# Placement matrices, norm rows and warm-up products of a mixture-of-experts stage set between the gate and up products

## The chip, the cores and the metric

One core of one Trainium2 chip runs the whole program. The metric is device time in microseconds (us) of one execution, lower is better. TensorE is called PE in the rows, its weight loads PEld, VectorE DVE, ScalarE ACT, GpSimd POOL, and the queue that issues the transfers SP.

## The reference, cut to what matters

Two post-norm layers over 512 tokens of width 1024. Layer 0 mixes tokens with attention, layer 1 with window pooling; each is followed by a mixture of 32 experts, where every token goes to two experts of one group of eight.

```python
for i in range(DEPTH):                       # DEPTH = 2
    mix = diff_attention(h, ...) if i % 2 == 0 else pool_mixer(h, ...)
    h = layer_norm(DEEPNORM_ALPHA * h + mix, ln_g[i, 0], ln_b[i, 0])
    ffn = hier_moe(h, ...)
    h = layer_norm(DEEPNORM_ALPHA * h + ffn, ln_g[i, 1], ln_b[i, 1])
...
def run_block(args):                         # one block of tokens of one expert
    xb, e = args
    h = jax.nn.silu(xb @ w_gate[e]) * (xb @ w_up[e])
    return h @ w_down[e]
...
out = jnp.zeros((N, D), x.dtype).at[tok_pad].add(y * w_pad[:, None])
```

## The kernel before

Each layer has a mixer stage and a mixture stage; the change is in the mixture stage, the function `moe` (lines 865 to 1250), which is called once for each layer. The 32 experts are taken as 16 pairs. An expert has 64 token slots, so a pair fills the 128 rows of a tile. The stage runs eight rounds, q = 0 to 7, of two pairs each (the loop at line 1160): the first pair of a round is p = 2q, the second p = 2q + 1. The order of PE's instructions in it is the order of the code (a manual schedule); DVE, ACT and POOL are ordered by a list scheduler that works on a cost model, so code that is moved on PE also moves work in their queues.

A pair goes through these steps. `gate_up` (L938) multiplies the gathered tokens `xT` with the gate weights into the PSUM bank psg and with the up weights into psu; ACT makes `sg`, the silu of psg (L945), DVE the product `h` with psu (L947). `flip` transposes h on PE (tp, L952), ACT copies it to hT (L953), and `down` (L963) multiplies it with the down weights into y. ACT (L972) and DVE (L973) split y, weighted by the slot weights `ws`, into a high and a low part `yy`. Later `spread_all` (L1130 to L1142) adds the rows back to their tokens: for each of 4 token tiles and 2 column halves a product of the placement matrix `Sm` with yy goes into a PSUM tile "sc" (four products for the two pairs of a round), and DVE adds the tile to the residual sum r (L1142). The spread of a round's two pairs stands in the next round, behind the gate and up products of its first pair: column half 0, then the flip, then column half 1.

`Sm` and `ws` of a pair come from `places` (L907): four transposes of the one-hot matrix G on PE (ga, L912), a copy by ACT to Sm (L913), four narrow products (pw, L916), and on DVE a copy pwc (L918) and two additions (L921). In this kernel both pairs of a round have this done one after the other, right ahead of the first pair's down product. Sm has three buffers. Behind the second pair's up product `gather2` makes the next round's G on DVE (L566, L567) and gathers its tokens on PE (L897) in four rounds of two column blocks, which ACT (L881) and DVE (L883) copy to xT; the flip stands between the second and the third of them.

Two more steps are rare. In round 0 `residue` (L1115) builds rows of the first norm's gains and shifts (row, L379) and scales r with them on DVE (L1121, L1123): four rows, behind the gather. In round 7 `norm_rows` (L383) builds four rows for the second norm, each copied by ACT to gb (L385), behind the spread.

PSUM has eight banks here: psg and psu (pool p0), and in pool p1 "ga", "tp" and the two banks of y, one buffer each; pool p2 has two buffers of the tag "sc". The gather's tiles go to "ga" and "tp" in turn, pw and the flip use "tp", the norm rows "sc" or "ga".

SP issues the weight transfers, 1 MB each, in the order of use; `fill` lets it run ahead by up to 14 units, and a transfer starts when the unit that it overwrites has been read.

`warm` (L302) is a helper that issues n products of constants, 128 x 256 in bf16, which nothing reads.

Of the kernel before, what the change touches and what calls it, by code (L numbers as in the profile page):

```python
# [8 lines left out]
F32 = mybir.dt.float32  # L9
F32R = mybir.dt.float32r  # L10
# [29 lines left out]
WARM3 = 24  # L40
WARM4 = 10
WARM2 = 2
REGION = {mybir.EngineType.PE, mybir.EngineType.DVE, mybir.EngineType.Activation, mybir.EngineType.Pool}
FILL2 = 3

# [19 lines left out]
def tile_trunk(ctx, tc, x, w_qkv, w_o, p_in, p_grp, p_scale, p_out,  # L65
# [804 lines left out]
    def moe(l, rt_in, name1, after):  # L870
        with ExitStack() as es:
# [13 lines left out]
            def gather(slots, cc, xT, pairs):  # L885

                n = pairs * P
                G = keep.tile([P, NT, 2 * P], F32R, name="G", tag="G")
                for j in range(NT):
                    do(place_in(G[:, j, 0:n], slots, cc, j))  # L890

                def round(k0, ga):
                    for k in range(k0, k0 + 2):
                        for j in range(NT):
                            g = G[:, j] if pairs == 2 else G[:, j:j + 1, 0:P].to_broadcast([P, 2, P])
                            for i in range(2):
                                PE.matmul(ga[:, k - k0], half_of(xs[j], i).bitcast(F32R)[:, k], g,  # L897
                                          start=j + i == 0, stop=j + i == NT)
                    for k in range(k0, k0 + 2):
                        factor(xT[:, k, 0:n], ga[:, k - k0, 0:n], k, (ACT, V)[k % 2])  # L900

                def ga_tile(k0):
                    return p1.tile([P, 2, 2 * P], F32, name="ga", tag=("ga", "tp")[k0 // 2 % 2])

                return G, [lambda k0=k0: round(k0, ga_tile(k0)) for k0 in range(0, KD, 2)]

            def places(G, i, wd, Sm, ws):  # L907

                ga = p1.tile([P, NT, P], F32, name="ga", tag="ga")
                gi = G[:, :, i * P:(i + 1) * P]  # L910
                for j, t in enumerate(tiles):
                    PE.transpose(ga[:, t], gi[:, j].bitcast(F32), ident)  # L912
                ACT.activation(Sm[:, :].rearrange("p (t q) -> p t q", t=NT), ga, AF.Copy)  # L913
                pw = p1.tile([P, 4], F32, name="pw", tag="tp")
                for t in range(NT):
                    PE.matmul(pw, gi[:, t], wd[:, t], start=t == 0, stop=t == NT - 1)  # L916
                pc = mo.tile([P, 4], F32, name="pwc", tag="pwc")
                V.tensor_copy(pc, pw)  # L918
                for e in range(2):
                    es_ = slice(e * CAP, (e + 1) * CAP)  # L920
                    V.tensor_tensor(ws[es_], pc[es_, e:e + 1], pc[es_, 2 + e:3 + e], op=OP.add)  # L921

            def run(todo):
                if todo:
# [133 lines left out]
            plc = {}  # L1058

            def place(G, p):  # L1060
                Sm = mo.tile([P, S], F32R, name="Sm", tag="Sm", bufs=3)
                ws = mo.tile([P, 1], F32, name="ws", tag="ws", bufs=3)
                places(G, p % 2, wd[:, :, p], Sm, ws)
                plc[p] = Sm, ws

            def seek(xT1, Sm1):

# [18 lines left out]
                V.tensor_scalar(rem, rem, 0.0, None, op0=OP.max)  # L1086
                G1, rounds = gather(sl, code, xT1, 1)
                do(rounds)
                places(G1, 0, wx, Sm1, ws1)

            def fetch(w, pr, u2):
                wv = w[l].rearrange("e (p k) n -> e p (k n)", p=P)
# [9 lines left out]
                        nc.sync.dma_start(u2[c][e], wv[bass.ds(pr[e], 1), :, :, c * 512:(c + 1) * 512]  # L1102
                                          .rearrange("a p k n -> (a p) k n"))

            def bank():
                return p1.tile([P, 512], F32, name="row", tag="ga")

            def whole(c):

                for j, t in enumerate(tiles):  # L1110
# [1 line left out]
                    hi, lo = [half_of(xs[j], i)[:, :, c * 64:(c + 1) * 64] for i in range(2)]  # L1112
                    nc.gpsimd.tensor_tensor(rq, hi, lo, op=OP.add)

            def residue(q, tag):  # L1115

                ps = norm_row(l, 0, q, p2.tile([P, 512], F32, name="row", tag=tag))
                for t in tiles:
                    r = tok(R, t)[:, q % 2 * 512:(q % 2 + 1) * 512]
                    if q < 2:  # L1120
# [9 lines left out]
            def spread_all(c, ys):  # L1130

                for t in range(NT):
                    spread_sum([(yr, Sm) for yr, Sm in ys], t, c)
# [7 lines left out]
                r = tok(R, t)[:, c * 512:(c + 1) * 512]  # L1141
                V.tensor_tensor(r, r, ps, op=OP.add)  # L1142

            def gate_of(p):
                h = h_tile()
                gate_up(xT[:, :, (p % 2) * P:(p % 2 + 1) * P],
                        [[take(nm, l, p, e) for e in range(2)] for nm in "gu"], h)
                done(8)
                return h

# [9 lines left out]
            for q in range(NPAIR // 2):  # L1160
                p, final = 2 * q, q == NPAIR // 2 - 1

                fill(CAPW)
                h = gate_of(p)
                if q == 0:
                    R = two("r")
                    whole(0)
# [2 lines left out]
                fill(CAPW)  # L1170
                if prev:
                    spread_all(0, prev)
                hT = hT_tile()
                flip(h, hT)
                if prev:
                    spread_all(1, prev)
                if final:
                    gb, rows_ = norm_rows(l, 1, bank)
                    do(rows_)
                place(G, p)  # L1180
                place(G, p + 1)
                prev = [down_of(p, hT, wdn)]

                p += 1
                fill(5 if final else CAPW)
                h = gate_of(p)
                wdn = [take("d", l, p, i) for i in range(2)]
                Sm, ws = plc[p]
                if final:
# [16 lines left out]
                else:  # L1206
                    fill(CAPW)
                    xT, (G, rounds) = gather2(p + 1)
                    rows_ = [lambda i=i: residue(i, "sc") for i in (0, 2, 1, 3)] if q == 0 else []
                    do(rounds[0:2])  # L1210
                    hT = hT_tile()
                    flip(h, hT)
                    do(rounds[2:4] + rows_)
                    prev.append(down_of(p, hT, wdn))


# [107 lines left out]
```

## Time and profile before

| what | before |
|---|---|
| device time, median of 3 runs | 1577.65 us (1576.52 to 1577.86) |
| the profiled execution | 1577.44 us, span 1575.7 us |
| mean granted TensorE clock | 0.968 of full speed |
| PE busy | 1463.4 us (93% of the span) |
| DVE, ACT, POOL busy | 623.4 us (40%), 366.9 us (23%), 82.0 us (5%) |
| HBM traffic | 285 GB/s over the span |

The span runs from the first to the last instruction of the profiled execution; the device time has 1.7 us around it. A busy share is the share of the span in which an engine executed something. The granted clock is 1.00 at 2.4 GHz and 0.50 at 1.2 GHz. The two mixture stages stand at about 310 to 875 us and 1031 to 1553 us.

### The profile page before, as it was taken

Reading aid. Unit: us, or ns where it says so; the run is one execution under the profiler, and the core shown is the slowest. Engines: PE = TensorE matmul, PEld = TensorE weight load, DVE = VectorE, ACT = ScalarE, POOL = GpSimd, SP = SyncE. Lnnn points to the kernel's source line nnn. Section 1 sums busy time; section 2 is a strip of 40 time slices with the busy share of each in tenths; the row PEclk is TensorE's granted clock in tenths of the full one; section 3 lists DMA queues with packets and bytes.
Section 4 is the critical chain, followed back from the end, with each engine's and each line's share of the span. In section 5 each row is a group of like instructions: output and inputs, shape, how many; then the busy total and the mean of one; then the engine's idle time right before and its main releaser. Section 6 shows DMA issues by size and latency. Waiting matters only on the chain. (4 is left out here: it accounts for less than half of the span.)

```text
span 1575.7 us, 18863 instructions
## 1 busy us (share of the span) xinstructions
PE 1463.4 (93%) x7477; PEld 840.2 (53%) x7477; DVE 623.4 (40%) x1441; ACT 366.9 (23%) x738; POOL 82.0 (5%) x52
## 2 busy tenths in 40 slices
PE   9999999998999999999998599998999999999993
PEld 7767777734544454445542377844455445444541
DVE  4366466643331322322233866653322213313216
ACT  4355464511111111111110423421111011111110
POOL 0000000320000000000000600230000000000001
PEclk9999999999999999999899799999999999999987
DMA  7111431677999999999866016467999999999921
GB/s 258 38 54 55 160 134 55 267 316 294 413 397 409 411 408 399 412 406 411 337 267 229 13 54 241 196 266 295 413 408 411 397 408 413 399 407 413 406 104 55
DMA packets 85570, 450.19 MB, mean 286 GB/s; under 512 B 10648, under 2 KB 20448, under 8 KB 36320
## 3 DMA queue, kind: packets, MB, share of 16 engines
q1 hardware_dynamic: 85472, 448.86, 71.3%
q8 instruction: 64, 1.05, 0.3%
q14 instruction: 34, 0.28, 0.1%
HBM read 446.74 MB, written 2.10 MB: 285 GB/s over the span
## 5 line engine op out<-in xcount | busy, mean ns | idle before, releaser
L963 PE MATMUL y<-w_d,hT 128*64 128x512 f32 x960 | 226.3, 627 | 0.0
L938 PE MATMUL psg<-w_g,xT 128*64 128x512 f32 x1024 | 225.2, 593 | 0.2 <-ACT xT L881 0.2
L938 PE MATMUL psu<-w_u,xT 128*64 128x512 f32 x1024 | 225.1, 592 | 0.0
L973 DVE SCALAR_TENSOR_TENSOR yy<-y,ws,yy 128x512 fp32r<-128x512 f32 x66 | 48.6, 737 | 397.1 <-ACT yy L972 382.4
L938 PEld LDWEIGHTS psu<-w_u,xT 128*64 128x64 f32 x1024 | 73.1, 137 | 146.6 <-issue 142.9
L938 PEld LDWEIGHTS psg<-w_g,xT 128*64 128x64 f32 x1024 | 72.9, 137 | 146.0 <-issue 141.6
L963 PEld LDWEIGHTS y<-w_d,hT 128*64 128x64 f32 x960 | 69.3, 144 | 132.9 <-issue 131.1
L897 PEld LDWEIGHTS ga<-G,xs 128*128 128x128 f32 x960 | 114.1, 188 | 12.2 <-issue 12.2
L897 PE MATMUL ga<-G,xs 128*128 128x256 f32 x960 | 119.7, 282 | 0.0
L945 ACT ACTIVATE sg<-psg 128x512 f32<-128x512 f32 x33 | 19.7, 597 | 425.2 <-PE psg L938 425.2
L1139 PE MATMUL sc<-yy,Sm 128*128 128x512 f32 x240 | 102.0, 425 | 6.6 <-DVE r L1142 6.0
L1142 DVE TENSOR_TENSOR r<-r,sc 128x512 f32<-128x512 f32 x128 | 85.9, 685 | 36.1 <-PE sc L1140 36.1
L947 DVE TENSOR_TENSOR h<-sg,psu 128x512 f32<-128x512 f32 x33 | 35.6, 1078 | 161.2 <-PE psu L938 150.4
L1140 PE MATMUL sc<-yy,Sm 128*128 128x512 f32 x240 | 94.9, 396 | 0.0
L283 PE MATMUL acc<-pc,xTh 128*128 128x512 f32 x192 | 77.2, 402 | 1.8 <-ACT pc L256 1.5
L284 PE MATMUL acc<-pc,xTh 128*128 128x512 f32 x192 | 76.6, 399 | 0.8 <-DVE pc L257 0.8
L285 PE MATMUL acc<-pc,xTl 128*128 128x512 f32 x192 | 77.1, 401 | 0.0
L883 DVE TENSOR_SCALAR xT<-ga,gcol 128x256 f32<-128x256 f32 (+1 forms) x60 | 32.1, 536 | 107.8 <-ACT xT L881 107.8
L881 ACT ACTIVATE xT<-ga,gcol 128x256 f32<-128x256 f32 (+1 forms) x60 | 33.4, 557 | 152.0 <-PE ga L897 152.0
L1139 PEld LDWEIGHTS sc<-yy,Sm 128*128 128x128 f32 x240 | 45.1, 188 | 41.8 <-DVE r L1142 22.1
L972 ACT ACTIVATE yy<-y,ws 128x512 fp32r<-128x512 f32 x66 | 45.2, 685 | 80.0 <-PE y L991 36.2
L953 ACT ACTIVATE hT<-tp 128x512 f32<-128x512 f32 x33 | 19.7, 598 | 182.3 <-PE tp L952 182.3
(299 smaller groups left out, 1907.0 us busy)
## 6 DMA issues: line engine op xcount, KB each, us to landing
w_g<-in_moe_w_gate_dram SPq DMA_DIRECT2D x128, 1024.0 KB
w_u<-in_moe_w_up_dram SPq DMA_DIRECT2D x128, 1024.0 KB
w_d<-in_moe_w_down_dram SPq DMA_DIRECT2D x128, 1024.0 KB
w_a<-in_attn_w_qkv_dram SPq DMA_DIRECT2D x16, 512.0 KB
x<-in_x_dram SPq DMA_DIRECT2D x8, 512.0 KB
w_v<-in_attn_w_qkv_dram SPq DMA_DIRECT2D x4, 1024.0 KB
w_wo<-in_attn_w_o_dram SPq DMA_DIRECT2D x4, 1024.0 KB
wx<-in_moe_w_gate_dram SPq DMA_DIRECT2D x4, 1024.0 KB
```

The source lines that it names most:

```text
L283: PE.matmul(acc, xhl(0, k), wh, start=start and j == 0, stop=False)
L284: PE.matmul(acc, xhl(0, k), wl, start=False, stop=False)
L285: PE.matmul(acc, xhl(1, k), wh, start=False, stop=stop and j == len(order) - 1)
L897: PE.matmul(ga[:, k - k0], half_of(xs[j], i).bitcast(F32R)[:, k], g, start=j + i == 0, stop=j + i == NT)
L938: PE.matmul(ps[es_], xT[:, k, es_], ws2[e][k // 4][:, k % 4], start=k == 0, stop=k == KD - 1)
L947: V.tensor_tensor(h[:, :, :].rearrange("s k q -> s q k"), r(sg), r(gu[1]), op=OP.mult)
L963: PE.matmul(y[es_, c], hT[:, k, es_], wd(e, k, c), start=k == 0, stop=k == 3)
L972: ACT.activation(yr[:, c], y[:, c], AF.Copy, scale=wslot)
L973: V.scalar_tensor_tensor(yr[:, 2 + c], y[:, c], wslot, yy[:, c], op0=OP.mult, op1=OP.subtract)
L1139: PE.matmul(ps, sm, yr[:, c], start=i == 0, stop=False)
L1140: PE.matmul(ps, sm, yr[:, 2 + c], start=False, stop=i == len(ys) - 1)
L1142: V.tensor_tensor(r, r, ps, op=OP.add)
```

## The change

The placement matrices of both pairs of a round are made between the gate and the up product of the first pair, through a hook that `gate_up` already had. The two sets of transposes go to two PSUM banks, "ga" and one of the two "sc" buffers, and the narrow products of both pairs share one tile, pw. The norm rows move to the same hook: `residue` rows 0 and 2 at the second pair of round 0, rows 1 and 3 at the first pair of round 1; the last norm's four rows, two at each pair of round 7, now in "sc". The gather's second and third tiles go to "sc", its first and fourth to "ga". At round 0, where there is nothing to spread, nine unread products stand ahead of the flip and five behind it.

```diff
@@ -40,6 +40,8 @@
 WARM3 = 24
 WARM4 = 10
 WARM2 = 2
+WARM5 = 9
+WARM6 = 5
 REGION = {mybir.EngineType.PE, mybir.EngineType.DVE, mybir.EngineType.Activation, mybir.EngineType.Pool}
 FILL2 = 3
 
@@ -900,25 +902,36 @@
                         factor(xT[:, k, 0:n], ga[:, k - k0, 0:n], k, (ACT, V)[k % 2])
 
                 def ga_tile(k0):
-                    return p1.tile([P, 2, 2 * P], F32, name="ga", tag=("ga", "tp")[k0 // 2 % 2])
+                    if k0 in (2, 4):
+                        return p2.tile([P, 2, 2 * P], F32, name="ga", tag="sc")
+                    return p1.tile([P, 2, 2 * P], F32, name="ga", tag="ga")
 
                 return G, [lambda k0=k0: round(k0, ga_tile(k0)) for k0 in range(0, KD, 2)]
 
-            def places(G, i, wd, Sm, ws):
-
-                ga = p1.tile([P, NT, P], F32, name="ga", tag="ga")
-                gi = G[:, :, i * P:(i + 1) * P]
+            def flip_places(G, i, Sm, ga):
+
                 for j, t in enumerate(tiles):
-                    PE.transpose(ga[:, t], gi[:, j].bitcast(F32), ident)
+                    PE.transpose(ga[:, t], G[:, j, i * P:(i + 1) * P].bitcast(F32), ident)
                 ACT.activation(Sm[:, :].rearrange("p (t q) -> p t q", t=NT), ga, AF.Copy)
-                pw = p1.tile([P, 4], F32, name="pw", tag="tp")
-                for t in range(NT):
-                    PE.matmul(pw, gi[:, t], wd[:, t], start=t == 0, stop=t == NT - 1)
-                pc = mo.tile([P, 4], F32, name="pwc", tag="pwc")
-                V.tensor_copy(pc, pw)
-                for e in range(2):
-                    es_ = slice(e * CAP, (e + 1) * CAP)
-                    V.tensor_tensor(ws[es_], pc[es_, e:e + 1], pc[es_, 2 + e:3 + e], op=OP.add)
+
+            def slot_weights(G, todo, pw):
+
+                for i, (wd, ws) in enumerate(todo):
+                    for t in range(NT):
+                        PE.matmul(pw[:, 4 * i:4 * i + 4], G[:, t, i * P:(i + 1) * P], wd[:, t],
+                                  start=t == 0, stop=t == NT - 1)
+                n = len(todo)
+                pc = mo.tile([P, 8], F32, name="pwc", tag="pwc")
+                V.tensor_copy(pc[:, 0:4 * n], pw[:, 0:4 * n])
+                for i, (wd, ws) in enumerate(todo):
+                    for e in range(2):
+                        es_ = slice(e * CAP, (e + 1) * CAP)
+                        V.tensor_tensor(ws[es_], pc[es_, 4 * i + e:4 * i + e + 1],
+                                        pc[es_, 4 * i + 2 + e:4 * i + 3 + e], op=OP.add)
+
+            def places(G, wd, Sm, ws):
+                flip_places(G, 0, Sm, p1.tile([P, NT, P], F32, name="ga", tag="ga"))
+                slot_weights(G, [(wd, ws)], p1.tile([P, 8], F32, name="pw", tag="tp"))
 
             def run(todo):
                 if todo:
@@ -1058,10 +1071,16 @@
             plc = {}
 
             def place(G, p):
-                Sm = mo.tile([P, S], F32R, name="Sm", tag="Sm", bufs=3)
-                ws = mo.tile([P, 1], F32, name="ws", tag="ws", bufs=3)
-                places(G, p % 2, wd[:, :, p], Sm, ws)
-                plc[p] = Sm, ws
+
+                for i in range(2):
+                    Sm = mo.tile([P, S], F32R, name="Sm", tag="Sm", bufs=3)
+                    ws = mo.tile([P, 1], F32, name="ws", tag="ws", bufs=3)
+                    plc[p + i] = Sm, ws
+                steps = [lambda i=i: flip_places(G, i, plc[p + i][0],
+                                                 p1.tile([P, NT, P], F32, name="ga", tag="ga") if i == 0 else
+                                                 p2.tile([P, NT, P], F32, name="ga", tag="sc")) for i in range(2)]
+                return steps + [lambda: slot_weights(G, [(wd[:, :, p + i], plc[p + i][1]) for i in range(2)],
+                                                     p1.tile([P, 8], F32, name="pw", tag="tp"))]
 
             def seek(xT1, Sm1):
 
@@ -1086,7 +1105,7 @@
                 V.tensor_scalar(rem, rem, 0.0, None, op0=OP.max)
                 G1, rounds = gather(sl, code, xT1, 1)
                 do(rounds)
-                places(G1, 0, wx, Sm1, ws1)
+                places(G1, wx, Sm1, ws1)
 
             def fetch(w, pr, u2):
                 wv = w[l].rearrange("e (p k) n -> e p (k n)", p=P)
@@ -1102,9 +1121,6 @@
                         nc.sync.dma_start(u2[c][e], wv[bass.ds(pr[e], 1), :, :, c * 512:(c + 1) * 512]
                                           .rearrange("a p k n -> (a p) k n"))
 
-            def bank():
-                return p1.tile([P, 512], F32, name="row", tag="ga")
-
             def whole(c):
 
                 for j, t in enumerate(tiles):
@@ -1112,9 +1128,9 @@
                     hi, lo = [half_of(xs[j], i)[:, :, c * 64:(c + 1) * 64] for i in range(2)]
                     nc.gpsimd.tensor_tensor(rq, hi, lo, op=OP.add)
 
-            def residue(q, tag):
-
-                ps = norm_row(l, 0, q, p2.tile([P, 512], F32, name="row", tag=tag))
+            def residue(q):
+
+                ps = norm_row(l, 0, q, p2.tile([P, 512], F32, name="row", tag="sc"))
                 for t in tiles:
                     r = tok(R, t)[:, q % 2 * 512:(q % 2 + 1) * 512]
                     if q < 2:
@@ -1141,10 +1157,12 @@
                 r = tok(R, t)[:, c * 512:(c + 1) * 512]
                 V.tensor_tensor(r, r, ps, op=OP.add)
 
-            def gate_of(p):
+            def gate_of(p, between=()):
+
                 h = h_tile()
                 gate_up(xT[:, :, (p % 2) * P:(p % 2 + 1) * P],
-                        [[take(nm, l, p, e) for e in range(2)] for nm in "gu"], h)
+                        [[take(nm, l, p, e) for e in range(2)] for nm in "gu"], h,
+                        todo=[lambda: do(between)], at=(KD - 1,))
                 done(8)
                 return h
 
@@ -1161,7 +1179,13 @@
                 p, final = 2 * q, q == NPAIR // 2 - 1
 
                 fill(CAPW)
-                h = gate_of(p)
+                if final:
+                    gb, rows_ = norm_rows(l, 1, lambda: p2.tile([P, 512], F32, name="row", tag="sc"))
+                else:
+                    rows_ = [lambda i=i: residue(i) for i in (0, 2, 1, 3)]
+                placed = place(G, p)
+                h = gate_of(p, placed if q == 0 else (placed + rows_[0:2] if final else
+                                                      placed + rows_[2:4] if q == 1 else placed))
                 if q == 0:
                     R = two("r")
                     whole(0)
@@ -1170,20 +1194,20 @@
                 fill(CAPW)
                 if prev:
                     spread_all(0, prev)
+                else:
+                    wps = p2.tile([P, 512], F32, name="wps", tag="sc")
+                    warm(wps, WARM5)
                 hT = hT_tile()
                 flip(h, hT)
                 if prev:
                     spread_all(1, prev)
-                if final:
-                    gb, rows_ = norm_rows(l, 1, bank)
-                    do(rows_)
-                place(G, p)
-                place(G, p + 1)
+                else:
+                    warm(wps, WARM6)
                 prev = [down_of(p, hT, wdn)]
 
                 p += 1
                 fill(5 if final else CAPW)
-                h = gate_of(p)
+                h = gate_of(p, rows_[2:4] if final else rows_[0:2] if q == 0 else ())
                 wdn = [take("d", l, p, i) for i in range(2)]
                 Sm, ws = plc[p]
                 if final:
@@ -1206,11 +1230,10 @@
                 else:
                     fill(CAPW)
                     xT, (G, rounds) = gather2(p + 1)
-                    rows_ = [lambda i=i: residue(i, "sc") for i in (0, 2, 1, 3)] if q == 0 else []
                     do(rounds[0:2])
                     hT = hT_tile()
                     flip(h, hT)
-                    do(rounds[2:4] + rows_)
+                    do(rounds[2:4])
                     prev.append(down_of(p, hT, wdn))
 
 
```

Queue of PE in round 2 of layer 0, behind the up product: the products of the spread (Sm times yy into the tiles sc; a number is the buffer's, and a wait names the engine that is waited for). Before:

```order
L1139 MATMUL sc_3795<-yy_3549,Sm_3498 128x512
L1140 MATMUL sc_3795<-yy_3549,Sm_3498 128x512
L1139 MATMUL sc_3795<-yy_3728,Sm_3515 128x512 [waits Activation_49]
L1140 MATMUL sc_3795<-yy_3728,Sm_3515 128x512 [waits DVE_49]
L1139 MATMUL sc_3801<-yy_3549,Sm_3498 128x512
L1140 MATMUL sc_3801<-yy_3549,Sm_3498 128x512
L1139 MATMUL sc_3801<-yy_3728,Sm_3515 128x512
L1140 MATMUL sc_3801<-yy_3728,Sm_3515 128x512
L1139 MATMUL sc_3807<-yy_3549,Sm_3498 128x512 [waits DVE_49]
```

The same place in the changed program:

```order
L1155 MATMUL sc_3835<-yy_3558,Sm_3383 128x512
L1156 MATMUL sc_3835<-yy_3558,Sm_3383 128x512
L1155 MATMUL sc_3835<-yy_3737,Sm_3385 128x512 [waits Activation_49]
L1156 MATMUL sc_3835<-yy_3737,Sm_3385 128x512 [waits DVE_49]
L1155 MATMUL sc_3841<-yy_3558,Sm_3383 128x512 [waits DVE_49]
L1156 MATMUL sc_3841<-yy_3558,Sm_3383 128x512
L1155 MATMUL sc_3841<-yy_3737,Sm_3385 128x512
L1156 MATMUL sc_3841<-yy_3737,Sm_3385 128x512
L1155 MATMUL sc_3847<-yy_3558,Sm_3383 128x512 [waits DVE_49]
```

The second tile had no wait and has one now; in both programs the third has one. In the program before, the tiles take the two "sc" buffers in turn and a tile's wait is for the addition of the tile two ahead of it; in the changed one all eight tiles of a round lie in one buffer, and the wait is for the addition of the tile just ahead.

Queue of ACT at the same place, from the copies of the gather to the next silu. Before:

```order
L945 ACTIVATE sg_3776<-psg_3742 128x512 [waits DVE_49,PE_49,Activation_49]
L972 ACTIVATE yy_3728<-y_3711,ws_3516 128x512 [waits DMAHW6_49,DMAHW7_49,DMAHW4_49,DMAHW1_49]
L972 ACTIVATE yy_3728<-y_3711,ws_3516 128x512 [waits DVE_49]
L953 ACTIVATE hT_3819<-tp_3820 128x512 [waits PE_49,Activation_49]
L913 ACTIVATE Sm_3850<-ga_3852 128x512 [waits PE_49]
L913 ACTIVATE Sm_3867<-ga_3869 128x512 [waits PE_49]
```

and in the changed program:

```order
L958 ACTIVATE sg_3816<-psg_3755 128x512 [waits DVE_49,PE_49,Activation_49]
L915 ACTIVATE Sm_3750<-ga_3772 128x512 [waits PE_49]
L985 ACTIVATE yy_3737<-y_3720,ws_3386 128x512 [waits DMAHW6_49,DMAHW7_49,DMAHW4_49,DMAHW1_49]
L985 ACTIVATE yy_3737<-y_3720,ws_3386 128x512 [waits DVE_49]
L966 ACTIVATE hT_3859<-tp_3860 128x512 [waits PE_49,Activation_49]
L915 ACTIVATE Sm_3752<-ga_3778 128x512 [waits PE_49]
```

The first copy to Sm now stands behind the silu; the second stayed behind the copy to hT, and waits there for the last spread product that reads the old Sm in its buffer.

Queue of DVE in round 0 of layer 0, from the end of the routing (MAX to ixi) to the product h of the first pair. Before:

```order
L1047 MAX m_3012<-rem 128x8
L1048 MAX_INDEX ix<-m_3012,rem 128x8
L1049 CAST ixf<-ix 128x2
L1050 CAST ixi<-ixf 128x2
L947 TENSOR_TENSOR h<-sg,psu 128x128x4
```

and in the changed program:

```order
L1061 MAX_INDEX ix<-m_3012,rem 128x8
L925 COPY pwc<-pw 128x8
L1062 CAST ixf<-ix 128x2
L568 TENSOR_SCALAR G<-cf,cc 128x256
L1063 CAST ixi<-ixf 128x2
L929 TENSOR_TENSOR ws<-pwc 64x1 x4
L569 SCALAR_TENSOR_TENSOR G<-cf,cc,G 128x256
L568 TENSOR_SCALAR G<-cf,cc 128x256 x2
L569 SCALAR_TENSOR_TENSOR G<-cf,cc,G 128x256 x2
L568 TENSOR_SCALAR G<-cf,cc 128x256
L569 SCALAR_TENSOR_TENSOR G<-cf,cc,G 128x256
L1015 TENSOR_SCALAR cc<-code 128x8
L960 TENSOR_TENSOR h<-sg,psu 128x128x4
```

The copy pwc, the additions to ws, all eight instructions of the next round's G and cc now stand ahead of h; before they stood behind it.

## Rows read from the trace of the kernel before

**Rows 1.** The page, part 1: busy time of the engines in the span.
```profile
PE 1463.4 (93%) x7477; PEld 840.2 (53%) x7477; DVE 623.4 (40%) x1441; ACT 366.9 (23%) x738; POOL 82.0 (5%) x52
```

**Rows 2.** Stretches: us, busy by engine, PEclk, DMA share, GB/s.
```profile
442.00:504.00 62.00, 60.12 (x316) 29.60 (x314) 16.22 (x33) 8.37 (x14) 0.00 (x0) 1.00 0.99 405
```

**Rows 3.** PE's waits: line, waited for, us in total, times, longest.
```profile
PE tp L952 <- DVE xT L883: 17.3, 14, 1.2
PE sc L1139 <- DVE r L1142: 6.0, 18, 1.2
```

**Rows 4.** Timeline, spread of round 2: start, duration, work, [idle before and releaser].
```profile
458.26 0.50 PE L1139 MATMUL sc<-yy,Sm 128*128 128x512 f32 x1 [0.30 <-DVE r L1142]
459.06 0.39 PE L1140 MATMUL sc<-yy,Sm 128*128 128x512 f32 x1
459.49 0.69 DVE L1142 TENSOR_TENSOR r<-r,sc 128x512 f32<-128x512 f32 x1 [0.69 <-PE sc L1140]
...
461.80 0.69 DVE L1142 TENSOR_TENSOR r<-r,sc 128x512 f32<-128x512 f32 x1 [0.67 <-PE sc L1140]
462.54 0.49 PE L1139 MATMUL sc<-yy,Sm 128*128 128x512 f32 x1
463.57 0.41 PE L1139 MATMUL sc<-yy,Sm 128*128 128x512 f32 x1
```

**Rows 5.** Timeline, places and down product of round 2.
```profile
464.50 0.60 PE L912 MATMUL ga<-cf,G 128*128 128x128 f32 x4
465.79 0.66 PE L912 MATMUL ga<-cf,G 128*128 128x128 f32 x4 [0.35 <-ACT Sm L913]
466.72 7.09 PE L963 MATMUL y<-w_d,hT 128*64 128x512 f32 x32
```

**Rows 6.** Timeline, first pair of layer 0.
```profile
316.72 7.04 PE L938 MATMUL psu<-w_u,xT 128*64 128x512 f32 x32
319.31 0.90 DVE L257 TENSOR_TENSOR wd<-wsum,wd 128x128 fp32r<-128x128 f32 x1 [0.39 <-ACT wd L256]
325.11 1.03 DVE L947 TENSOR_TENSOR h<-sg,psu 128x512 f32<-128x512 f32 x1
326.20 0.66 PE L952 MATMUL tp<-cf,h 128*128 128x128 f32 x4 [2.44 <-DVE h L947]
330.11 9.25 PE L963 MATMUL y<-w_d,hT 128*64 128x512 f32 x32
330.22 0.16 DVE L918 COPY pwc<-pw 128x4 f32<-128x4 f32 x1 [1.10 <-PE pw L916]
333.65 0.17 DVE L1002 TENSOR_SCALAR cc<-code 128x8 f32<-128x8 f32 x1
```

**Rows 7.** Groups of instructions by line: busy us, mean ns of one.
```profile
L302 PE MATMUL acc<-cb 128*128 128x256 bf16 x12 | 2.0, 275 | 0.0
```

**Rows 8.** Timeline, norm rows of rounds 0 and 7 of layer 0.
```profile
362.54 1.95 PE L379 MATMUL row<-vec,cf 72*128 72x128 f32 x16
363.80 2.47 DVE L1121 SCALAR_TENSOR_TENSOR r<-r,row 128x512 f32<-128x512 f32 x4
366.42 1.13 PE L379 MATMUL row<-vec,cf 72*128 72x128 f32 x8 [1.93 <-DVE r L1121]
370.79 9.39 PE L963 MATMUL y<-w_d,hT 128*64 128x512 f32 x32
...
774.34 1.06 PE L379 MATMUL row<-vec,cf 72*128 72x128 f32 x8
776.08 1.16 PE L379 MATMUL row<-vec,cf 72*128 72x128 f32 x8 [0.69 <-ACT gb L385]
786.67 9.66 PE L963 MATMUL y<-w_d,hT 128*64 128x512 f32 x32
```

**Rows 9.** Stretches of 5 us, columns as in rows 2.
```profile
774.00:779.00 5.00, 3.63 (x25) 3.16 (x24) 0.98 (x2) 1.19 (x2) 0.00 (x0) 0.92 1.01 393
869.00:874.00 5.00, 3.35 (x12) 1.27 (x8) 4.05 (x7) 3.94 (x5) 2.11 (x1) 1.00 0.00 0
```

## The prediction

> **What bounds the kernel now.** I read the page's engine line first: PE is busy 1463.4 us of a span of 1575.7 [rows 1], so the time is PE's work and PE's waits. Then a table of stretches. In the mixture stage a round of two pairs takes 62.0 us again and again (round 2 to round 6); PE is busy 60.12 of them at clock 1.00, and the transfers have a share of 0.99 [rows 2]. So PE sets the pace there, with the transfers close behind; none of PE's waits is for a transfer. The list of those waits shows what can be won in a round: 17.3 us in 14 waits of the flip for the gather's copies, and only 6.0 us of the spread for DVE [rows 3]. The timelines then show each place that the change touches. The sum is made against the profiled execution, 1577.44 us, which is 0.2 us under the median of the runs.
>
> **The change, part by part** (costs for one layer; it is made in both).
>
> *Spread.* This is the largest term, and no line of the diff names it. Sm has three buffers. The new Sm of both pairs are now wanted ahead of the up product, but the two of the round before are read until the spread ends. So the second new Sm has no buffer until then: ACT's queue holds its copy behind hT. Its source, the second ga, meanwhile keeps one of the two "sc" buffers. All eight tiles of the spread go through the other, and PE's queue shows a wait for DVE from the second tile on, where there was none before the third. The price of one such turn is read from the tile at 458.26, which started after a wait: its fourth product ends at 459.06 + 0.39 = 459.45, DVE adds from 459.49 for 0.69 to 460.18, and PE starts 0.05 after an addition ends (461.80 + 0.69 = 462.49, next tile at 462.54): 460.23 - 458.26 = 1.97 us a tile [rows 4]. What waits for the spread's first addition starts at 458.26; today that is the third tile, and it will be the second. The eighth then starts 6 x 1.97 later, at 470.08, and not at 463.57: +6.5 us. Rounds 1 to 7 have such a spread: 7 x 6.5 = **+45.5 us**. The flip fits into one of the gaps. Nothing covers the rest, since PE's next work, the down product, is queued behind the spread. Bounds: the smallest wait of a tile in the rows is 0.30 us, 7 x 7 x 0.30 = 15 us; the upper end is the clock's fall (below). I take 1.97, because every piece of it is measured on these instructions.
>
> *What the pauses do to the clock.* In the stretch 774 to 779 PE was busy 3.63 us of 5, with pauses of 0.69 us only, and its granted clock fell from 1.00 to 0.50 near the end (mean 0.92). From 869 to 874 PE ran spread products with waits for DVE, was busy 3.35 of 5, and kept 1.00 [rows 9]. The new spread, 1.19 us busy in 1.97, is the second kind: the same products, the same waits. I take 1.00. The Trainium skill, "TensorE: Matmul & The Clock Gate", section "A second HAM failure mode: psum-queue depth-cycling", speaks against this: it tells of a kernel that cycles through PSUM banks with small idle spots between groups of products, whose clock swings between its two levels. By the rows above the sum has no term for it and ends at 1629 us; by that page it would be the first rival, 1731 us.
>
> *Places.* From the first transposes at 464.50 to the down product at 466.72 it takes 2.22 us [rows 5], of which 0.35 is PE's wait for the first Sm. In the new place two banks and one pw tile need no such wait; the other 1.9 us stay on PE. Saved 0.35 us in rounds 1 to 6: **-2.1 us** (round 7 is counted below).
>
> *Gather.* Its second and third tile now lie in "sc", so the flip's bank is free: 7 x 1.24 us = **-8.7 us** [rows 3]. The bank it takes is free by then, since the second Sm is copied a whole pair earlier.
>
> *First pair.* Two things get late. The narrow products need wd, which DVE has at 319.31 + 0.90 = 320.21, while the gate product ends at 316.72, where up starts today, and the transposes take 0.7: PE waits 2.8 us, and up, which ends at 316.72 + 7.04 = 323.76 today, will end near 328.1. And DVE's queue now has pwc, ws, all of G and cc ahead of h. They take 3.6 us today (330.22 to 333.82), with two more additions 3.9, so h starts at 325.11 + 3.9 = 329.0, the flip at 330.1 and not 326.20 [rows 6]. A flip of 0.66 and an ACT copy with its two hand-overs, 0.69 in [rows 8], put down's start near 331.5, not 330.11. The nine products fill 1.5 of the 2.0 us for which PE then waits, at 2.0 / 12 = 0.17 us each [rows 7]. I take it that the clock stays up: then down takes 7.09 us [rows 5] and not 9.25 [rows 6]. Together **-0.7 us**, not the five or so that a covered wait would give.
>
> *Rows of round 0.* Today they take 8.25 us, 362.54 to 370.79, and the clock falls: down needs 9.39 [rows 8], 2.3 more than at 1.00. Now two rows stand at the second pair, 1.95 us with no wait. The other two meet round 1, where one "sc" buffer is held: the second waits until DVE has done pwc, ws and a first part of G (about half of the 3.6 us above, 1.8) and four scalings (2.47), less the first row's own 1.06: a stall of some 3.3 us. That is 1.95 + 2.1 + 3.3 = 7.35, so -0.9, and -3.2 if the clock holds there. It fell after waits of 1.93 and less, so I take even odds: **-2.0 us**.
>
> *Rows of round 7.* Today 774.34 to 786.67, 12.33 us with the places, and down at 9.66, 2.57 too long [rows 8]: 14.9. Now 1.9 of places, 2 x 1.06 + 1.95 of rows, and one wait: the first copy to gb stands behind the silu, an Sm and both yy on ACT. It is at least the 0.69 of today and, where the 3.3 of round 0 is the worst stall of this kind, at most that; I take 1.6. That is 7.6, so -7.3; with even odds on a fall that costs 2.3: **-6.1 us**.
>
> Sum: 45.5 - 2.1 - 8.7 - 0.7 - 2.0 - 6.1 = +25.9 a layer, +51.8 in all: 1577.4 + 51.8 = **1629 us**. A round of the middle goes from 62.0 to 62.0 + 6.5 - 0.35 - 1.24 = 66.9 us, so the transfers get slack and bind nothing.
>
> **Rivals.**
> *The clock falls in the spreads.* For it: the stretch from 774, where shorter pauses were enough, four us after they began [rows 9]. Against it: 869 to 874. If so, some five of the eight tiles stream at half speed, about 0.94 us more each, and down takes 2.6 more, as after the rows of round 7 [rows 8]: 7.3 us x 14 = 102, about 1731 us. Chance 0.15.
> *The unread products do not do their work.* They cover only part of the two us at the first pair, and if the clock falls there as today, down costs 2.2 more in each layer: 1633 us. For it: today 2.44 us were enough [rows 6]. Against it: here PE is idle for less. Chance 0.08.
> *The spread does not pay* (the other side). If "sc" came free early in the spread, as soon as the second Sm is copied, two tiles would be in flight as today, and only the savings would stay: -19.6 a layer, 1538 us, or up to 19 more where the transfers at share 0.99 [rows 2] cannot follow the six shorter rounds. The point that decides is 19.6 / 7 = 2.8 us for one spread: under that the change wins. Against it: the order of ACT's queue and the one buffer are fixed in the program. Chance 0.05.
>
> **How the numbers follow.** The forecast, 1629 us, has 0.72. The range holds it and the second rival, 0.80. Its lower end has spreads that cost 5.5 and not 6.5 (-14), a clock that holds at both sets of rows (-5), and some 7 us less for places and first pairs: 1603. Its upper end has the clock falling in four of the 14 spreads (+29) and at the rows and first pairs (+10): 1668. Left out are the first and the third rival. A change of under 0.2% (3.2 us) cannot be told from none. Slower is the forecast and the first two rivals, 0.95; the third gives 0.04 faster and 0.01 for a balance near nothing.
>
> **What would show it.** After: waits of the spread for DVE near 14 x 7 x 0.8 = 78 us where 6.0 stood; the flip's waits for the gather gone; rounds of 67 us with clock 1.00 and a smaller share of transfers; the first pair's h about 4 us later. I am wrong if tiles of a spread start less than 1.5 us apart, or if the clock is under 1.00 in the spreads.

## The result and the profile after

The changed kernel takes 1668.9 us (median of 4 runs, 1663.51 to 1676.09) against 1577.09 for the kernel before: 5.8% slower, ratio 1.0583 with a 95% interval of 1.0559 to 1.0606. The forecast was 1629 us with a range up to 1668, so the sign was right, the loss was forecast at 52 us and is 92, and the time lies just above the range. The profiled execution of the changed kernel is the shortest of its four, 1663.5 us with a span of 1661.6.

The page, part 1, busy time of the engines, beside [rows 1]:

```profile
PE 1504.1 (91%) x7505; PEld 843.5 (51%) x7505; DVE 621.8 (37%) x1425; ACT 364.2 (22%) x738; POOL 81.9 (5%) x52
```

PE is busy for 40.7 us more, though the change adds only 28 products that nothing reads. Its waits, beside [rows 3] (line, waited for, us in total, times, longest):

```profile
PE sc L1155 <- DVE r L1158: 74.4, 92, 1.3
...
PE row L381 <- DVE r L1137: 6.2, 2, 3.1
...
PE row L381 <- ACT gb L387: 3.9, 2, 2.0
PE pw L921 <- DVE wd L259: 3.5, 2, 2.4
PE tp L965 <- DVE h L960: 2.6, 3, 1.3
```

The flip's 17.3 us of waiting for the gather are gone, as forecast. In their place stand 74.4 us of waits of the spread for DVE, where 6.0 stood. The 14 spreads of the span, seven a layer, take 238 us where they took 124: 68 us more of waits, and 46 more of busy time (elsewhere PE is busy for 5 us less), in part because the products of a tile no longer run into those of the next, and in part because the clock falls. What is saved elsewhere, the flip's waits above all, brings the growth of the span down to 85.9 us. The timeline of PE in the spread of round 2 shows both parts (start, duration, work, idle time before and who ended it); four products make a tile:

```profile
460.85 0.50 PE L1155 MATMUL sc<-yy,Sm 128*128 128x512 f32 x1
...
463.28 0.50 PE L1155 MATMUL sc<-yy,Sm 128*128 128x512 f32 x1 [1.25 <-DVE r L1158]
...
465.26 0.50 PE L1155 MATMUL sc<-yy,Sm 128*128 128x512 f32 x1 [0.78 <-DVE r L1158]
...
467.24 0.61 PE L1155 MATMUL sc<-yy,Sm 128*128 128x512 f32 x1 [0.78 <-DVE r L1158]
467.65 0.63 PE L1156 MATMUL sc<-yy,Sm 128*128 128x512 f32 x1
...
468.93 1.05 PE L965 MATMUL tp<-cf,h 128*128 128x128 f32 x4
469.91 0.79 PE L1155 MATMUL sc<-yy,Sm 128*128 128x512 f32 x1
...
470.92 0.40 PE L1155 MATMUL sc<-yy,Sm 128*128 128x512 f32 x1
...
472.34 0.50 PE L1155 MATMUL sc<-yy,Sm 128*128 128x512 f32 x1 [0.78 <-DVE r L1158]
```

Tiles start 465.26 - 463.28 = 1.98 us apart: the turn that was forecast at 1.97 from [rows 4]. From 467.2 to 470.8 most products last about 0.63 and not 0.40 us: the granted clock is down. The queue of ACT says who holds the other "sc" buffer, since the second copy to Sm, which reads it, starts only behind the spread's last products (it waits for the product at L1156):

```profile
470.08 0.60 ACT L966 ACTIVATE hT<-tp 128x512 f32<-128x512 f32 x1 [10.84 <-PE tp L965]
477.06 0.60 ACT L915 ACTIVATE Sm<-ga 128x512 fp32r<-128x512 f32 x1 [6.38 <-PE sc L1156]
```

A table of stretches, one row for the spread of rounds 1 to 4 (us, busy time by engine, granted clock, share of the transfers, GB/s), where the kernel before needs 8.85 us at 1.00 each time:

```profile
393.80:409.30 15.50, 10.01 (x40) 5.95 (x40) 6.37 (x9) 1.01 (x2) 0.00 (x0) 1.00 0.53 224
460.80:477.40 16.60, 11.45 (x38) 6.90 (x36) 6.38 (x9) 0.94 (x2) 0.00 (x0) 0.90 0.68 281
529.00:547.30 18.30, 13.16 (x38) 7.88 (x37) 6.36 (x9) 1.20 (x2) 0.00 (x0) 0.78 0.61 255
599.90:617.50 17.60, 12.44 (x40) 7.59 (x38) 6.38 (x9) 1.00 (x2) 0.00 (x0) 0.81 0.65 271
```

The first is the forecast itself: +6.65 us at a clock of 1.00. In the others the same tiles with the same waits run partly at 1.2 GHz. In round 3 the fall reaches into the down product behind the spread, which takes 7.09 us at 1.00:

```profile
547.30 8.11 PE L976 MATMUL y<-w_d,hT 128*64 128x512 f32 x32
```

The norm rows that moved to round 1 also lose what they were to gain. PE and DVE there:

```profile
378.45 1.14 PE L381 MATMUL row<-vec,cf 72*128 72x128 f32 x8
...
380.06 2.48 DVE L1137 SCALAR_TENSOR_TENSOR r<-r,row 128x512 f32<-128x512 f32 x4
...
382.68 2.04 PE L381 MATMUL row<-vec,cf 72*128 72x128 f32 x8 [3.09 <-DVE r L1137]
...
384.65 9.22 PE L951 MATMUL psu<-w_u,xT 128*64 128x512 f32 x32
```

The second row waits 3.09 us for the first one's scalings, and the up product behind takes 9.22 and not 7.04 us. In round 7 the second row waits 1.96 us for ACT's copy, and the up product takes 8.78.

At the first pair of layer 0 the flip no longer waits 2.44 us [rows 6], but PE waits as long for wd, and then up runs long (in layer 1 the wait for wd is 1.11 us, and up takes 7.09):

```profile
319.44 1.05 PE L921 MATMUL pw<-wd,G 128*128 128x4 f32 x8 [2.36 <-DVE wd L259]
320.42 8.79 PE L951 MATMUL psu<-w_u,xT 128*64 128x512 f32 x32
329.14 1.16 PE L304 MATMUL wps<-cb 128*128 128x256 bf16 x9
330.45 0.66 PE L965 MATMUL tp<-cf,h 128*128 128x128 f32 x4 [0.15 <-DVE h L960]
...
331.79 7.09 PE L976 MATMUL y<-w_d,hT 128*64 128x512 f32 x32
```

### The profile page after: what moved, and what is told of

Same layout as the page of the kernel before. It is cut to its first block, busy times and chain, and to the rows that moved or that the text cites. A ratio compares the mean times of both kernels' runs of the same rounds, so it can differ in the third digit from the quotient of the medians.

```text
span 1661.6 us, 18913 instructions
## 1 busy us (share of the span) xinstructions
PE 1504.1 (91%) x7505; PEld 843.5 (51%) x7505; DVE 621.8 (37%) x1425; ACT 364.2 (22%) x738; POOL 81.9 (5%) x52
## 5 line engine op out<-in xcount | busy, mean ns | idle before, releaser
L951 PE MATMUL psu<-w_u,xT 128*64 128x512 f32 x1024 | 235.5, 614 | 0.0
L976 PE MATMUL y<-w_d,hT 128*64 128x512 f32 x960 | 217.7, 607 | 0.3
L1155 PE MATMUL sc<-yy,Sm 128*128 128x512 f32 x240 | 120.8, 503 | 75.3 <-DVE r L1158 74.4
L1155 PEld LDWEIGHTS sc<-yy,Sm 128*128 128x128 f32 x240 | 51.5, 215 | 140.4 <-DVE r L1158 120.7
L1156 PE MATMUL sc<-yy,Sm 128*128 128x512 f32 x240 | 106.8, 445 | 0.0
L985 ACT ACTIVATE yy<-y,ws 128x512 fp32r<-128x512 f32 x66 | 45.2, 685 | 144.6 <-DVE yy L986 93.2
```

Source lines behind the costliest of these rows:

```text
L951: PE.matmul(ps[es_], xT[:, k, es_], ws2[e][k // 4][:, k % 4], start=k == 0, stop=k == KD - 1)
L976: PE.matmul(y[es_, c], hT[:, k, es_], wd(e, k, c), start=k == 0, stop=k == 3)
L985: ACT.activation(yr[:, c], y[:, c], AF.Copy, scale=wslot)
L1155: PE.matmul(ps, sm, yr[:, c], start=i == 0, stop=False)
L1156: PE.matmul(ps, sm, yr[:, 2 + c], start=False, stop=i == len(ys) - 1)
```

## Experiments

The theory was that the loss is the held "sc" buffer and nothing else of the change; the rivals were that the late copy or the steps in their new places cost the time, and, for what the sum had missed, that the clock falls for another reason than the pauses.

**The held buffer given back.** The second matrix goes to the bank of the first, which nothing else needs until the gather:

```diff
-  p1.tile([P, NT, P], F32, name="ga", tag="ga") if i == 0 else
-  p2.tile([P, NT, P], F32, name="ga", tag="sc")) for i in range(2)]
+  p1.tile([P, NT, P], F32, name="ga", tag="ga")) for i in range(2)]
```

> The changed kernel with one edit: the second placement matrix of a round is transposed into the bank "ga", like the first, and no longer into one of the two "sc" buffers. Its copy to Sm still stands behind hT on ACT and still waits for the end of the spread. Theory A (the loss is the held "sc" buffer): the 14 spreads take 8.85 us each as in the kernel before and not 15.0 to 18.4, PE's waits of the spread for DVE fall from 74.4 to about 6 us, the clock stays at 1.00 in them; 1668.9 - 114 (spreads) - 3 (down products behind them) + 5 (14 waits of 0.35 us for the copy of the first matrix) = about 1557 us, 1550 to 1563. Theory B (as A, but then the transfers, at a share of 0.99 before, set the pace of five rounds a layer at 62.0 us again): about 1570 to 1577 us. Theory C (the late copy itself or the moved steps cost the time, whichever bank is held): above 1640 us.

Measured: 1556.82 us, ratio to the kernel before 0.986 (0.9838 to 0.9882). PE's waits, and ACT's second copy behind the spread of round 2:

```profile
PE ga L914 <- ACT Sm L915: 16.9, 16, 4.2
PE sc L1154 <- DVE r L1157: 5.5, 17, 0.5
```

```profile
459.64 0.60 ACT L966 ACTIVATE hT<-tp 128x512 f32<-128x512 f32 x1 [6.72 <-PE tp L965]
462.96 0.60 ACT L915 ACTIVATE Sm<-ga 128x512 fp32r<-128x512 f32 x1 [2.72 <-PE sc L1155]
```

The copy still waits for the spread's products, as in the changed kernel, and the 14 spreads are back at 8.84 to 9.11 us with the clock at 1.00. So theory A holds: the late copy by itself costs the spread nothing, the bank that it holds makes the loss. The row's wait in round 1 went too: there all 16 products of two rows now run in one stretch of 2.03 us, and the up product takes 7.09. The price is a new wait of PE for the copy of the first matrix, 0.69 us a round where 0.35 had been allowed, and 4.2 at the first pair of layer 0. There that copy stands on ACT behind the silu and its table load, and these behind a copy for wd, for which ACT waits 4.97 us.

**The gather's banks alone, in the kernel before.**

```diff
-  return p1.tile([P, 2, 2 * P], F32, name="ga", tag=("ga", "tp")[k0 // 2 % 2])
+  if k0 in (2, 4):
+      return p2.tile([P, 2, 2 * P], F32, name="ga", tag="sc")
+  return p1.tile([P, 2, 2 * P], F32, name="ga", tag="ga")
```

> The kernel before with one edit of the change alone: the second and third tile of the gather lie in "sc", the first and fourth in "ga". If PE sets the pace: the 14 waits of the flip for the gather's copies go, 9.57 - 8.14 = 1.43 us a round by the changed kernel's trace, 1577.1 - 20 = 1557 us, with a middle round at 60.6 us. If the transfers set it as soon as a round is under 62.0 us: only the rounds outside the middle gain, 1571 to 1577 us, and a new wait for a transfer shows on PE.

Measured: 1554.97 us, ratio 0.985 (0.9834 to 0.9867). Two rounds of the middle take 121 us, 60.6 each. One such stretch:

```profile
501.00:561.00 60.00, 59.34 (x312) 29.39 (x310) 16.22 (x33) 8.31 (x14) 0.00 (x0) 1.00 1.01 418
```

PE sets the pace, and none of the waits of its products is for a transfer: the transfers follow at 418 GB/s, where [rows 2] had 405 at a share of 0.99. A share near 1 was no proof of a bound there.

**The pauses filled.** Four unread products behind six of the eight tiles, in the changed kernel:

```diff
   for t in range(NT):
       spread_sum([(yr, Sm) for yr, Sm in ys], t, c)
+      if len(ys) == 2 and t < NT - 1:
+          warm(p1.tile([P, 512], F32, name="wpf", tag="tp"), 4)
```

> The changed kernel with one edit: behind each of the tiles 1, 2, 3, 5, 6 and 7 of a two-pair spread stand four unread products (128x256, bf16, 0.17 us each), in the pause of 0.78 us in which PE waits for DVE. The spread stays in one bank. Theory: the pauses lower the clock, which is what the sum left out. Then tiles stay 1.97 us apart, all spreads take 15.0 to 15.6 us and none 16.6 to 18.4, the downs behind them 7.09 and not 8.11: 1668.9 - 21 - 4 = about 1644 us, 1638 to 1650. Rival: the clock falls there for another reason, or the unread products do not hold it: 1663 to 1676 us, or more if they delay the tiles.

Measured: 1642.25 us (1639.56 to 1644.15), ratio to the kernel before 1.0407 (1.0387 to 1.0426). The tiles in round 2:

```profile
465.09 0.50 PE L1157 MATMUL sc<-yy,Sm 128*128 128x512 f32 x1 [0.79 <-DVE r L1160]
...
466.13 0.61 PE L304 MATMUL wpf<-cb 128*128 128x256 bf16 x4
467.07 0.50 PE L1157 MATMUL sc<-yy,Sm 128*128 128x512 f32 x1 [0.33 <-DVE r L1160]
...
469.05 0.51 PE L1157 MATMUL sc<-yy,Sm 128*128 128x512 f32 x1 [0.33 <-DVE r L1160]
```

The spread of round 3, which took 18.35 us at 0.78:

```profile
529.70:545.20 15.50, 12.73 (x64) 7.84 (x64) 6.36 (x9) 1.05 (x2) 0.00 (x0) 1.00 0.74 308
```

Tiles stay 1.98 us apart, all 14 spreads take 15.0 to 15.5 us and every down product behind them 7.09. Products that nothing reads, added to a slower kernel, win 26.7 us back and narrow its scatter from 12.6 to 4.6 us (four runs each). The tiles, the bank and the turn are unchanged, and only the pauses are filled: the idle pauses are what lowers the clock in these spreads.

**The unread products of round 0 left out** of the changed kernel (`WARM5 = 0`, `WARM6 = 0`).

> The changed kernel without the nine and five unread products of round 0. If they hold the clock there: the down product of each layer's first pair takes about 9.2 us and not 7.09, +4 us in all, less 0.2. If the work around them holds it anyway: 7.09 us without them too. The time itself cannot tell 4 us from the scatter of this kernel (1663 to 1676); the length of these two down products can.

Measured: 1676.76 us in the one run, which lies within 1 us of the longest run of the changed kernel and says nothing about the time. The first pair's down product in layer 0 and in layer 1:

```profile
333.11 7.09 PE L976 MATMUL y<-w_d,hT 128*64 128x512 f32 x32 [0.69 <-ACT hT L966]
...
1096.97 8.45 PE L976 MATMUL y<-w_d,hT 128*64 128x512 f32 x32 [0.69 <-ACT hT L966]
```

Neither expectation holds alone: layer 0 does without them, layer 1 loses 1.36 us.

**A better order.** To the first experiment's kernel: the narrow products between the two sets of transposes, and in round 0 "sc" for the second matrix.

```diff
-  p1.tile([P, NT, P], F32, name="ga", tag="ga") if i == 0 else
-  p2.tile([P, NT, P], F32, name="ga", tag="sc")) for i in range(2)]
+  p2.tile([P, NT, P], F32, name="ga", tag="sc") if i and p == 0 else
+  p1.tile([P, NT, P], F32, name="ga", tag="ga")) for i in range(2)]
...
+  return [steps[0], weights, steps[1]] if p else steps + [weights]
```

> The kernel of the first experiment with two edits: from round 1 on the narrow products stand between the two sets of transposes, so that PE has work while ACT copies the first matrix; in round 0, where no Sm is waited for, the second matrix goes to "sc" as in the changed kernel. Against the first experiment the first pairs should take 29.7 and 27.7 us again and not 34.0 and 31.5 (-8 in all), and the first pair of a middle round 31.6 - 0.4 = 31.2 and not 32.4 us (12 x 1.2 = -14). If PE sets the pace: 1557 - 22 = 1535 us, 1530 to 1540. If the transfers do by now (in the first experiment the weighted copies of round 7's first pair waited some 7.5 us for a transfer): that wait grows by what is won before it, and the time stays at 1547 to 1557 us.

Measured: 1532.51 us (1531.11 to 1533.53), ratio 0.9718 (0.9699 to 0.9737), 2.8% faster than the kernel before. PE between gate and up of round 2, and the whole of that round:

```profile
440.04 0.66 PE L914 MATMUL ga<-cf,G 128*128 128x128 f32 x4
440.45 1.03 PE L921 MATMUL pw<-wd,G 128*128 128x4 f32 x8
441.38 0.66 PE L914 MATMUL ga<-cf,G 128*128 128x128 f32 x4
```

```profile
433.10:493.60 60.50, 60.20 (x316) 29.33 (x314) 15.96 (x32) 8.22 (x14) 0.00 (x0) 1.00 1.01 416
```

No wait is left in the places, and PE is busy for 60.20 of 60.50 us: PE still sets the pace, as the first case of the expectation has it. The first pair of a middle round takes 31.6 us, though, and not the 31.2 hoped for: that is what the kernel before needs. The steps are as long between gate and up as ahead of the down product. One loss is left, in round 7 of layer 0, whose second pair takes 52.8 us and 45.2 before. There DVE makes h before the G of an extra item (a block of tokens beyond the 64 slots of an expert), and PE waits for that G:

```profile
PE ga L899 <- DVE G L569: 4.2, 1, 4.2
```

**The rows in their old places**, in the fifth experiment's kernel (the calls of `residue` behind `do(rounds[2:4])`, those of `norm_rows` behind `spread_all(1, prev)`, as before).

> The kernel of the fifth experiment with the norm rows back where the kernel before has them: those of round 0 behind the gather, those of round 7 behind the spread. If PE sets the pace the rows cost again what they did: about 10.6 us in round 0 (8.25 and a down product 2.3 longer) for 4.1, and 12.9 us in round 7 (10.3 with waits and 2.6) for 4.1: 6.5 + 8.8 = 15 us a layer, so about 30 us more than the fifth. If the transfers set the pace of a layer, the moved rows bring little: within 6 us of the fifth.

Measured: 1552.78 us, ratio to the kernel before 0.9839 (0.9818 to 0.986): 20.3 us more than the fifth. The rows' new places are worth something once no buffer is held. It is not the 30 us of the first case, mostly because of that last pair of layer 0: it takes 45.6 us here, 7.2 less than in the fifth kernel.

**One bank for the spread, in the kernel before**, and nothing else moved.

```diff
-  ps = p2.tile([P, 512], F32, name="sc", tag="sc")
+  ps = (p1.tile([P, 512], F32, name="sc", tag="ga") if len(ys) == 2 else
+        p2.tile([P, 512], F32, name="sc", tag="sc"))
```

> The kernel before with one edit: the tiles of a two-pair spread lie in the one buffer "ga", which is idle then, and not in the two "sc" buffers. Nothing else moves, and nothing is held. Theory: this alone is the loss of the changed kernel. 14 spreads of 15.5 us and not 8.85 give +93 us, the fall of the clock in them, as in the changed kernel, about +25 more: 1577 + 118 = 1695 us, 1668 (no fall) to 1702. Rival (the changed kernel's spreads suffer from what was moved around them, on DVE or ACT, as much as from the bank): under 1640 us.

Measured: 1739.98 us (1737.21 to 1747.8), ratio 1.1049 (1.1016 to 1.1081). The bank alone makes the loss, so the rival falls; but the size was missed by 45 us. The 14 spreads themselves take 114 us more than in the kernel before, close to the 118 expected; the miss lies in what stands behind them. The end of the spread of round 3, with what follows it:

```profile
553.73 0.50 PE L1140 MATMUL sc<-yy,Sm 128*128 128x512 f32 x1 [0.78 <-DVE r L1143]
...
555.71 0.66 PE L912 MATMUL ga<-cf,G 128*128 128x128 f32 x4 [0.78 <-DVE r L1143]
...
557.05 0.66 PE L912 MATMUL ga<-cf,G 128*128 128x128 f32 x4 [0.34 <-ACT Sm L913]
...
557.98 8.78 PE L963 MATMUL y<-w_d,hT 128*64 128x512 f32 x32
```

Here the places stand right behind the spread, in the same bank, with two more pauses, and 13 of the 14 down products behind them take 8.0 to 9.7 us, where 12 of 14 took 7.09 in the kernel before. In the changed kernel the places have left that spot, and 8 of the 12 down products behind the spreads of rounds 1 to 6 take 7.09, the other four 8.11.

**The unread products once more**, left out of the fifth experiment's kernel.

> The kernel of the fifth experiment without the nine and five unread products of round 0. In the changed kernel without them (fourth experiment) the down product of the first pair took 7.09 us in layer 0 and 8.44 in layer 1. If it goes like that here: -0.4 us of products, +1.4 in layer 1, so 1532 to 1535 us, no difference that can be told. If the products are what holds the clock in both layers: two downs of about 8.4 to 9.2 us, +3 to +4 us: 1536 us.

Measured: 1532.12 us, ratio 0.9713 (0.9697 to 0.9729), the same as with them. Both first pairs' down products take 7.09 us, but the up product of layer 1's first pair takes 8.61, and 7.09 in the fifth kernel. So the products win nothing that these runs can tell; where the clock falls in a first pair differs between these traces.

## Why the prediction came out too low, and which step failed

Measured against forecast, us for a layer (lengths from the starts of the gate products in both traces):

| term | forecast | layer 0 | layer 1 |
|---|---|---|---|
| spreads of rounds 1 to 7 | +45.5 | +57.9 | +56.1 |
| down products behind them, rounds 1 to 6 | 0 | +2.0 | +2.0 |
| places, rounds 1 to 6 | -2.1 | -1.0 | -1.0 |
| gather | -8.7 | -10.0 | -10.0 |
| first pair | -0.7 | +0.3 | -1.2 |
| rows of round 0 | -2.0 | -0.1 | 0.0 |
| round 7 without its spread | -6.1 | -3.5 | -5.0 |
| sum | +25.9 | +45.6 | +40.9 |

*Spread.* The mechanism of the term was right in every step: the buffer, the late copy, the turn of 1.97 us, the +6.5 us (6.65 in round 1). "What the pauses do to the clock" is the step that failed: "I take 1.00", and "the sum has no term for it". One of the prediction's own signs of being wrong, "the clock is under 1.00 in the spreads", came true. The prediction took 1.00 from the stretch 869 to 874 [rows 9], because the same products with the same waits had kept it there. But that stretch has some three us of them, behind which PE has no work, and in the four us ahead of it PE was busy throughout, as its row of the kernel before shows:

```profile
865.00:869.00 4.00, 4.00 (x19) 1.48 (x17) 3.87 (x7) 0.00 (x0) 0.00 (x0) 1.00 0.80 262
```

A new spread has 15 us of them. The other row, 774 to 779, where the clock fell with shorter pauses, was the nearer one: PE was busy for 3.63 of 5 us in it, and is for 1.19 of 1.97 in the new turn. Here the clock fell in 11 of 14 spreads. It cost some 21 us in them and 4 in four down products behind them: 25 of the 34 us between the forecast and the profiled execution. The third experiment gives 26.7. Of the other 9 us, some 4 are the rows of round 0, 4 round 7, 2 the turn of 1.98 and 2 the places; the gather gave 3 more than forecast.

*First rival.* The clock falls in the spreads, 1731 us: half right, and its chance of 0.15 was too small. The fall came, but for the length of some one to three tiles and not five, and most down products behind were spared: 25 us and not 102. The Trainium skill, "TensorE: Matmul & The Clock Gate", section "A second HAM failure mode: psum-queue depth-cycling", which spoke for it, tells of short idle spots between groups of products under which the clock swings between its two levels. These traces agree: the granted clock was 0.78 to 0.90 in such spreads, and 1.00 with the pauses filled. That kernel cycles through banks; here all 14 spreads of the kernel before, which alternate between two banks with pauses of some 0.3 us, kept 1.00.

*Rows.* The stall in round 1 was there, 3.09 us where 3.3 were forecast, but the even odds on the clock were too kind: up took 2.2 us more in round 1 in both layers, and 1.7 more in round 7. Both waits were further costs of the held bank: in the first experiment they are gone in all four places. There up takes 7.09 in three of them and 8.13 in round 7 of layer 1, where one wait of 0.69 us, the one for the copy of the first matrix, stands ahead of the fall; the same wait in the other rounds had no fall behind it, and why this one had is not shown.

*First pair.* The term came out near, but by luck and not by its steps: PE waited for wd, 2.36 us in layer 0 and 1.11 in layer 1 where 2.8 were forecast, and in layer 0 the clock then fell in up, not in down. Whether the unread products hold it in down is not settled: without them it held in three of the four first pairs looked at.

*Gather, places, transfers.* As forecast, within 1.3 us a layer, though the places gave half of their 2.1; the second experiment gives 23 us for the gather's banks alone, at transfers for which PE does not wait. *The spread does not pay*: its condition, an "sc" that comes free early, did not hold in the changed kernel. The first and the fifth experiment make it true another way, by not taking "sc" from round 1 on, and win 1.4% and 2.8%, 1556.8 and 1532.5 us where the rival had 1538 to 1557.

*Range.* Its upper end gave four of 14 spreads a fall, at 7.3 us each: 29 us. In fact 11 fell, at some 2.3 us each: 25 us. That the time came so near the upper end is luck, two errors that cancel: too few falls, each at too high a price. The profiled execution even lies inside. With one row each way on the clock, a fall in all 14 had to be in the range. The other executions of the changed kernel are up to 12.6 us longer than the profiled one, and their granted clock is lower (0.956 at 1663.5 us, 0.946 at 1676.1), which points the same way; where it fell in them is not shown.

Left open: why the same pauses lower the clock at different tiles from round to round, and in three spreads not at all (round 1 of both layers, round 7 of layer 1). Their place in the program does not settle it: in the trace of the fourth experiment, whose spreads have the same tiles and waits, round 2 of layer 0 kept 1.00 (15.50 us) and round 1 of layer 1 fell to a mean of 0.72 (19.08 us). A fourth buffer for Sm, which would take away the late copy itself, was not tried.

## What to carry to other kernels

When a step is moved earlier, count how many copies of its result are then alive, and follow the copy that finds no buffer back to its source: whatever PSUM bank the source lies in is lost until the copy can run, to everyone who shares it. A loop of product and addition in one bank costs the sum of both engines and not the larger (here 1.19 and 0.69 us and two hand-overs, 1.98 a tile), and the pauses may cost the clock besides. Price a fall of the clock over the whole length of the new pauses, not from a short stretch that happened to keep it.

## What was not expected of the hardware

The same spread, tile for tile, ran 15.51, 16.64, 18.35 and 17.63 us in rounds 1 to 4, by the clock alone, and layer 1 repeats the four to within 0.02 us. Unread products that cut its pauses from 0.78 to 0.33 us kept PE at 2.4 GHz in all 14. The transfers, at a share of 0.99 and 405 GB/s, gave 418 when PE asked for more.
